# A hybrid delta-rule and attention layer: Q/K norm and turn written later, squares moved to GpSimd, clearing products, two loads reordered

## Chip, cores and metric

One core of a Trainium2 chip runs the whole layer. The metric is the device time of one execution in microseconds (us), the median over several runs; the 128-partition engines are TensorE (PE; its weight loads are PEld), VectorE (DVE), ScalarE (ACT), GpSimd (POOL) and SyncE (SP), which issues most of the DMAs.

## What is computed

The input x is 2048 tokens of 1024 float32 values. It is normalised and multiplied by one wide matrix; the columns feed a gated delta rule (four heads of 128) and a dilated attention (eight heads of 64, three dilations); both are gated, concatenated, multiplied by an output matrix and added to x. Cut to the parts that the change touches:

```python
def rms_norm(x, w):
    xf = x.astype(jnp.float32)
    return xf * lax.rsqrt(jnp.mean(xf * xf, axis=-1, keepdims=True) + EPS) * w.astype(jnp.float32)

def dilated_attention_branch(qkv, gate, q_norm_w, k_norm_w, rel_bias):
    q, k, v = jnp.split(qkv, 3, axis=-1)
    q = rms_norm(split_heads(q, ATT_HEADS), q_norm_w) * (ATT_HEAD_DIM ** -0.5)
    k = rms_norm(split_heads(k, ATT_HEADS), k_norm_w)
    ...
    return o * jax.nn.silu(gate.astype(jnp.float32))

def hybrid_layer(x, norm_w, w_in, ...):
    h = rms_norm(x, norm_w).astype(x.dtype)
    proj = h @ w_in
    ...
    return x + mixed @ w_out
```

## The kernel before

**Products in three parts.** Every projection is done as three products of split operands: a rounded high part (`xh`, `wh`) and the rest (`xl`, `wl`). ACT makes the high parts, DVE the rests by a subtraction of two tiles in SBUF.

**The opening (lines 218 to 342).** The first column block is multiplied as the data come in, in eight rounds, one for each 128 rows of x (`kt`). In a round ACT makes `xh` and one or two `wh` and squares the x tile (`x_square`, lines 256 to 264); DVE makes `xl` (`x_low`), one or two `wl` (`z_low`) and adds the square to the running sum `acc` (`x_add`); PE does twelve products into four banks of PSUM (`pz`); SP issues the next loads. `x_square` is used for all four blocks of 512 tokens (`tb`); in the opening it works on block 0. POOL does one small power at line 226 and is then free until the sums of squares are raised to -1/2 (`x_norm`, line 291). Everything from line 218 to line 379 is pinned: each engine gets its instructions in the order in which they are written.

**The middle (lines 380 to 778)** is not pinned. A planner puts the instructions of the projections, the triangular inverses and the delta rule in order by their priorities (`PATT0`, `PGATE` and the like) and by its own account of times; each engine's order is fixed when the program is built.

**The Q, K and V projection (`proj_fill`, lines 881 to 955)** is a generator that writes one product per call, 2304 in all, counted by `n`. Two token tiles share one bank of the ring `pj`, which has two (`PJB`), so a bank takes 48 products, and the product 48 after its end is the first to need the same bank again. For Q and K, three things follow the last product of a bank: `post_sums` at once (ACT squares, DVE sums, and POOL adds and raises `ss` to -1/2), `post_norm` 24 products later (DVE reads the bank, multiplies by `ss` and so frees it), and `post_turn` another 18 later (PE turns four 128x128 tiles into the single bank `pm`, ACT scales them, two DMAs of the ACT queue write them out). This part is pinned too. Its first 960 products are taken before the attention starts and are planned in among the delta rule; the others are written between the pieces of the attention, nine, nine and eight per step (`step`, lines 1275 to 1287). A step also writes DVE's work on scores, copies and weights; POOL's queue holds the reordering of keys and queries (`keys`, `queries`) and the blending of the three patterns (`blend`), in the order written.

**The output projection (`out_fill`, lines 1354 to 1442)** is the generator for steps 48 to 97. Its jobs are numbered; `load` (line 1370) issues a job's load ahead, and for attention parts only once `ready` has the quarter that it needs, which line 1266 adds at a step and a place in it. `res_load` at lines 1427 to 1429 brings back, for the last five token tiles, the sums that were stored earlier. All of these are issues on SP's queue, which waits in order.

The line of a product or of an ACT instruction in a pinned part is 99 in the profile, that of the helper which writes them; such rows are told apart by their tiles.

Of the kernel before, what the change touches and what calls it, by code (L numbers as in the profile page):

```python
# [16 lines left out]
P = 128  # L17
# [67 lines left out]
def hybrid(tc, xT, x, norm_w, w_in, conv_w, a_log, dt_bias, dn_norm_w, q_norm_w, k_norm_w,  # L85
# [135 lines left out]
    adma = nc.scalar.dma_start  # L221
    adma(nw, norm_w)
    nc.vector.memset(one, 1.0)
    warm = sp0.tile([P, 4], F32, name="warm")
    nc.scalar.activation(warm, mhalf[:, :4], AF.Silu)
    nc.gpsimd.tensor_tensor(warm, phalf, mhalf[:, :4], op=ALU.pow)
# [29 lines left out]
    def x_square(n):  # L256
        tb, kt = divmod(n, KT)
        if kt == 0:
            acc[tb] = sp0.tile([P, 512], F32, name="acc", bufs=2)
            nc.scalar.activation(acc[tb], xraw[n], AF.Square)  # L260
        else:
            sq = sp0.tile([P, 512], F32, name="sq", bufs=2)
            nc.scalar.activation(sq, xraw[n], AF.Square)
            acc[tb, kt] = sq

    def x_low(n):
        tb, kt = divmod(n, KT)
# [76 lines left out]
    n = KT  # L344
# [536 lines left out]
    def proj_fill():  # L881

        raws = w_load(0)
        cur = w_split(raws[0]) + w_split(raws[1])
        posts = []
        n = 0
        for s_ in range(12):
            hf, i = divmod(s_, 6)
            g2, w = SETS[i]
            nxt = []  # L890
            for o8 in range(8):
                tt = hf * 8 + o8
                if o8 % 2 == 0:
                    ps = psA.tile([P, 512], F32, name="pj", bufs=PJB)

                nx = s_ * 8 + o8 - 44
                if nx in (0, 4):
                    alloc_x(2 + nx // 4, xp0)
                if nx == -4:
                    for k in range(3):  # L900
                        x_load(k)
                if nx == -1:
                    x_load(3)
                    x_load(4)

                if s_ < 11:
                    if o8 == 1:
                        raws = w_load((i + 1) % 6)
                    if o8 == 5:
                        nxt = w_split(raws[0])  # L910
                else:
                    if o8 == 1:
                        rs = [w_out_load(k) for k in range(2)]
                    if o8 == 4:
                        wo_tiles(0)
                    if o8 >= 4:
                        wo_split(o8 - 4, rs[o8 - 4])
                        if o8 < 6:
                            rs.append(w_out_load(o8 - 2))
                tb, o = divmod(tt, 4)  # L920
                c0 = tt % 2 * 256
                for kt in range(KT):
                    if 0 <= nx < 8 and kt % 4 == 0:
                        k = 2 * nx + kt // 4
                        x_split(k)
                        if k < 11:
                            x_load(k + 5)
                    for x_, w_ in ((xh, 0), (xh, 1), (xl, 0)):
                        while posts and posts[0][0] <= n:
                            posts.pop(0)[1]()  # L930
                        if s_ < 11 and o8 == 7 and kt == 2 and w_ == 0 and x_ is xh:
                            nxt += w_split(raws[1])
                        m = nc.tensor.matmul(ps[:, c0:c0 + 256], x_[tb][:, kt, o * P:(o + 1) * P],
                                             cur[kt][w_][:, cur[kt][2], :256], start=kt == 0 and x_ is xh and w_ == 0,
                                             stop=kt == KT - 1 and x_ is xl)
                        if n == HOLD * 192:
                            tc.add_manual_dep(m.ins, mark["pe"].ins.name, NOSYNC, reason="behind the delta rule")
                        n += 1
                        yield
                if tt % 2:  # L940
                    t0 = tt - 1
                    if w == 2:
                        post_v(g2, t0, ps)
                    else:
                        ss = post_sums(t0, ps)

                        def norm(ps=ps, ss=ss, w=w, g2=g2, t0=t0):
                            qn = post_norm(ps, ss)
                            posts.append((n + 18, lambda: post_turn(w, g2, t0, qn)))
                            posts.sort(key=lambda a: a[0])  # L950
                        posts.append((n + 24, norm))
                        posts.sort(key=lambda a: a[0])
            cur = nxt
        while posts:
            posts.pop(0)[1]()
# [278 lines left out]
    def at_step(t, where, f, *args):  # L1234
        todo.setdefault((t, where), []).append((f, args))
# [3 lines left out]
    for i, g in enumerate(G):  # L1239
        b = 12 * i  # L1240
        if i:
            at_step(b - 4, 1, g["load"])
        at_step(b - (2 if i else 3), 1, g["queries"], 0)
        for k in range(1, 6):
            at_step(b + 2 * k - 3, 0, g["queries"], k)
        at_step(b, 0, g["keys"], 1)
        at_step(b + 4, 0, g["keys"], 2)
        for j, t, where in (((0, -1, 0), (2, 1, 0), (4, 3, 0), (5, 4, 0), (6, 6, 0), (7, 7, 2), (8, 8, 0), (10, 10, 0))
                            if i < 4 else
                            ((0, 0, 0), (2, 1, 2), (4, 3, 2), (5, 4, 0), (6, 6, 0), (7, 7, 2), (8, 8, 0), (9, 9, 2),  # L1250
                             (10, 10, 0), (11, 11, 2))):
            at_step(b + t, where, g["vload"], j)
        at_step(b + 12, 1, g["sums"])
        at_step(b + 12, 2, g["sums_out"])
        if i < 7:
            at_step(b + 13, 2, g["sums_back"], 0, dma)
            at_step(b + 14, 0, g["sums_back"], 1, dma)
            at_step(b + 15, 1, g["weigh"])
            at_step(b + 15, 2, g["weigh2"])
            at_step(b + 16, 0, g["factors"])  # L1260
            for qd in range(4):
                d = i < 6
                at_step(b + 16 + qd + d, 0 if d else 2, g["blend_load"], qd)
                at_step(b + 17 + qd + d, 0 if d else 1, g["blend"], qd, nc.gpsimd)
                at_step(b + 19 + qd + d, 0 if d else 1, g["mixed"], qd)
                at_step(b + 20 + qd + 2 * d, 0, ready.add, (i // 4, i % 4, qd))
        else:
            at_step(b + 13, 0, g["sums_back"], 0, dma)
            at_step(b + 13, 1, g["sums_back"], 1, dma)
# [84 lines left out]
    def out_fill():  # L1354
# [48 lines left out]
        for i, (tt, kind, n, mm, buf) in enumerate(jobs):  # L1403
            if mm is None:
                continue
            nth += 1
            first, last = mm
            todo_ = []
            while i + 1 + len(todo_) < len(jobs):
                todo_.append(i + 1 + len(todo_))  # L1410
                if jobs[todo_[-1]][3]:
                    break
            if first:
                res = RES[tt] if kind == "att" else res_load(tt, x)
                po = [None, None]
            m = 0
            for b in range(2):
                if first:
                    po[b] = psX.tile([P, 512], F32, name="po", bufs=3)
                for _ in products(po[b], ops, b, first, last):  # L1420
                    m += 1
                    if nth < 2 and m in (8, 16):
                        k = 2 * nth + m // 8 - 1
                        wo_split(4 + k, RAW[k])
                    if m >= 3 * n and m % 3 == 0 and todo_:
                        nxt = split(todo_.pop(0))
                    if nth in range(18, 23) and m == 3 * n + 8:
                        k = nth - 18
                        RES[Q2[k]] = res_load(Q2[k], acc_d, K0[:, k * D:(k + 1) * D] if k < 2 else None)
                    if m >= 4:  # L1430
                        load(i + 3 if nth < 24 else i + 5)
                    if m == 3 * n + 4 and store:
                        dma(*store)
                        store = None
                    yield
                if last:
                    cs_ = slice(b * 512, (b + 1) * 512)
                    nc.vector.tensor_tensor(res[:, cs_], po[b], res[:, cs_], op=ALU.add)
            assert not todo_
            ops = nxt  # L1440
            if last and not (kind == "att" and n == 3):
                store = ((out if kind == "att" else acc_d)[tt * P:(tt + 1) * P, :], res)
# [77 lines left out]
```

## Time and profile before

| what | value |
|---|---|
| median of 3 runs | 1446.1 us (1442.88 to 1447.8) |
| the profiled execution, own time | 1442.2 us |
| its span, first to last instruction | 1440.4 us |
| busy: PE / DVE / ACT / POOL | 1374.0 / 897.2 / 680.1 / 427.2 us |
| mean granted clock of TensorE | 0.987 of full speed |
| chain that ended last, by engine | PE 61%, DVE 15%, DMA 11%, ACT 5%, issue 4%, POOL 2% |

The profiled execution lies 3.9 us under the median of the runs, so sums are made against its 1442.2 us and then carried to the median. In rows of the timeline the first number is the start and the second the duration, both in us; x4 is a count of merged instructions, and a bracket holds the idle time of the engine before the row and what ended it.

### The profile page before, as it was taken

What the parts mean: (1) busy time and instruction counts of PE and PEld (TensorE: products, weight loads), DVE (VectorE), ACT (ScalarE), POOL (GpSimd) and SP (SyncE); (2) the same over time, 40 slices, a digit from 0 to 9 for tenths busy, and PEclk for the clock granted to TensorE, in tenths of its full rate; (3) what the DMA queues carried; (4) which work ended last, traced back from release to release, by engine and by line L of the source; (5) the groups of instructions that cost most, each with busy time, mean ns of one, the idle gap of its engine ahead of it and who ended that gap; (6) DMA issues with size and microseconds to landing.
All of it is one profiled execution on the core that took longest, in us unless ns stands there. A gap on an engine that the chain in (4) does not pass through costs nothing.

```text
span 1440.4 us, 28745 instructions
## 1 busy us (share of the span) xinstructions
PE 1374.0 (95%) x10234; PEld 1223.6 (85%) x10234; DVE 897.2 (62%) x2786; ACT 680.1 (47%) x1937; POOL 427.2 (30%) x499
## 2 busy tenths in 40 slices
PE   7999999999998998999999899999998999999988
PEld 7998777777877887999999889999887778888877
DVE  6526678799894365777777554544354645466455
ACT  7634436642221333444444476665555545555520
POOL 0000000000002112442432523657466274655500
PEclk9999999999999999999999999999998999999999
DMA  7653445773557556566554554464448574755764
GB/s 218 165 117 70 99 102 133 156 132 55 116 88 193 147 83 171 133 166 168 133 143 76 124 127 116 100 174 119 112 118 246 146 247 134 216 154 171 200 175 150
DMA packets 301154, 205.00 MB, mean 142 GB/s; under 512 B 149283, under 2 KB 271027, under 8 KB 300500
## 3 DMA queue, kind: packets, MB, share of 16 engines
q1 hardware_dynamic: 233924, 171.70, 48.6%
q10 hardware_dynamic: 67088, 31.47, 7.9%
q8 instruction: 81, 1.33, 0.4%
q14 instruction: 61, 0.50, 0.1%
HBM read 142.61 MB, written 60.50 MB: 141 GB/s over the span
## 4 chain that ended last, share of the span: by engine, by line
PE 61%; DVE 15%; DMA 11%; ACT 5%; issue 4%; POOL 2%; SPq 1%; ACTq 0%; DVEq 0%; POOLq 0%
PE pj L99 13%; PE po L99 8%; PE pz L99 5%; PE sc L99 5%; PE pj L206 4%; PE pj L207 4%; PE pj L208 4%; PE pv L99 3%; PE pt L99 3%; DVE cy L473 3%; DVE inv L540 2%; DMA kT<-cv 2%; PE C L714 2%; PE SU L720 2%; ACT pr L99 2%
## 5 line engine op out<-in xcount | busy, mean ns | idle before, releaser
L99 ACT ACTIVATE pr<-pr,ml 128x192 f32<-128x192 f32 (+2 forms) x384 | 156.8, 410 | 161.6 <-DVE ml L99 161.6
L99 PE MATMUL pj<-wh,xh 128*128 128x256 f32 (+1 forms) x776 | 227.7, 293 | 0.0
L99 PE MATMUL pj<-wl,xh 128*128 128x256 f32 (+1 forms) x776 | 227.6, 293 | 0.0
L99 PE MATMUL pj<-wh,xl 128*128 128x256 f32 (+1 forms) x776 | 225.8, 291 | 0.0
L208 PE MATMUL pj<-xh,wl 128*128 128x512 f32 x512 | 203.9, 398 | 3.6 <-DVE wl L192 3.6
L206 PE MATMUL pj<-xh,wh 128*128 128x512 f32 x512 | 203.9, 398 | 1.3 <-ACT cy L475 1.2
L207 PE MATMUL pj<-xl,wh 128*128 128x512 f32 x512 | 203.2, 397 | 0.0
L99 PEld LDWEIGHTS pj<-wl,xh 128*128 128x128 f32 x776 | 148.3, 191 | 0.6 <-issue 0.4
L99 PEld LDWEIGHTS pj<-wh,xl 128*128 128x128 f32 x776 | 148.3, 191 | 0.0
L99 PEld LDWEIGHTS pj<-wh,xh 128*128 128x128 f32 x776 | 148.1, 191 | 0.2
L99 DVE CUSTOM_DVE_ANT_0 pr<-sc,bias 128x192 f32<-128x192 f32 (+2 forms) x384 | 100.1, 307 | 71.0 <-PE sc L99 70.2
L208 PEld LDWEIGHTS pj<-xh,wl 128*128 128x128 f32 x512 | 96.6, 189 | 27.3 <-DVE wl L192 5.3
L206 PEld LDWEIGHTS pj<-xh,wh 128*128 128x128 f32 x512 | 96.8, 189 | 24.4 <-ACT cy L475 1.6
L473 DVE SCALAR_TENSOR_TENSOR cy<-cu,cw,cy 128x512 f32<-128x512 f32 x144 | 107.9, 752 | 15.2 <-ACT cy L471 13.6
L207 PEld LDWEIGHTS pj<-xl,wh 128*128 128x128 f32 x512 | 96.6, 189 | 21.9
L99 POOL COPY qz<-q 64x512 f32<-64x512 f32 x96 | 92.5, 964 | 57.7 <-PE sc L99 54.7
L657 POOL MEMSET at__4520<- 64x256 f32 x1 | 0.3, 304 | 354.5 <-PE pj L207 354.5
L99 DVE COPY pT<-pt 64x128 f32<-64x128 f32 (+2 forms) x220 | 69.3, 323 | 56.4 <-PE pt L99 53.1
L99 PE MATMUL po<-xh,mhh 128*128 128x512 f32 x212 | 88.8, 419 | 3.9 <-ACT mhh L99 3.9
L99 PE MATMUL pv<-pT,V 128*64 128x128 f32 (+1 forms) x1328 | 79.1, 269 | 9.8 <-DVE pT L99 4.7
L99 PE MATMUL po<-xl,mhh 128*128 128x512 f32 x212 | 88.1, 415 | 0.0
L99 PE MATMUL po<-xh,mhl 128*128 128x512 f32 x212 | 87.7, 414 | 0.3 <-DVE mhl L99 0.3
(360 smaller groups left out, 3151.8 us busy)
## 6 DMA issues: line engine op xcount, KB each, us to landing
wraw<-in_w_in SPq DMA_DIRECT2D x44, 512.0 KB, 6.9
cv<-cy ACTq DMA_DIRECT2D x48, 256.0 KB, 2.7
Fb<-F SPq DMA_DIRECT2D x64, 192.0 KB, 5.7
xr<-in_xT SPq DMA_DIRECT2D x32, 256.0 KB, 4.5
kT<-cv SPq DMA_DIRECT2D x32, 256.0 KB, 3.3
qk<-qs ACTq DMA_DIRECT2D x64, 128.0 KB, 3.3
res<-in_x SPq DMA_DIRECT2D x13, 512.0 KB, 5.2
V<-v_d SPq DMA_DIRECT2D x20, 256.0 KB, 6.2
```

The lines of the kernel that those rows point to most:

```text
L99: i = f(*args, **kw)
L206: nc.tensor.matmul(ps, wh[:, k, c * P:(c + 1) * P], xh[tb][:, kt, :], start=kt == 0, stop=False)
L207: nc.tensor.matmul(ps, wh[:, k, c * P:(c + 1) * P], xl[tb][:, kt, :], start=False, stop=False)
L208: nc.tensor.matmul(ps, wl[:, k, c * P:(c + 1) * P], xh[tb][:, kt, :], start=False, stop=kt == KT - 1)
L473: nc.vector.scalar_tensor_tensor(y, u[:, i:i + 512], cw[:, ct, i:i + 1], y, op0=ALU.mult, op1=ALU.add)
L540: nc.vector.tensor_tensor(pr_[:, :i, :i], Tt[:, :i, :i], L[:, None, :i, i].to_broadcast([P, i, i]), op=ALU.mult)
L657: nc.gpsimd.memset(at_[:CH, :, :CH], 0.0)
L714: nc.tensor.matmul(pc[:, s_], g["WQ"][:, u, s_], S0[:, s_], start=True, stop=True)
L720: nc.tensor.matmul(su[:, s_], g["Ks"][:, u, s_], VN, start=True, stop=True)
```

## The change

Five edits. (1) DVE clears 128 columns of `rstd_b`, and 14 products of these zeros by themselves go into a bank of PSUM at the start, into no result. (2) `x_square` runs on POOL for block 0, eight squares in all, and on ACT for the others as before. (3) In `proj_fill` the norm is written 30 products after the bank's end, where it was 24, and the turn 24 after the norm, where it was 18. (4) For the last head pair but one (`i == 6`) `ready` is added at the end of the step before, three products earlier. (5) The fifth of the reloads of stored sums is written at the 24th job of the output projection (`nth` 23), where it was at the one before.

```diff
     nc.vector.memset(one, 1.0)
+    nc.vector.memset(rstd_b[:, :P], 0.0)
+    pm = psA.tile([P, 512], F32, name="pm", bufs=1)
+    for _ in range(14):
+        nc.tensor.matmul(pm[:, :P], rstd_b[:, :P], rstd_b[:, :P], start=True, stop=True)
...
         if kt == 0:
-            acc[tb] = sp0.tile([P, 512], F32, name="acc", bufs=2)
-            nc.scalar.activation(acc[tb], xraw[n], AF.Square)
+            acc[tb] = sq = sp0.tile([P, 512], F32, name="acc", bufs=2)
         else:
-            sq = sp0.tile([P, 512], F32, name="sq", bufs=2)
+            acc[tb, kt] = sq = sp0.tile([P, 512], F32, name="sq", bufs=2)
+        if tb == 0:
+            nc.gpsimd.tensor_tensor(sq, xraw[n], xraw[n], op=ALU.mult)
+        else:
             nc.scalar.activation(sq, xraw[n], AF.Square)
-            acc[tb, kt] = sq
...
-                            posts.append((n + 18, lambda: post_turn(w, g2, t0, qn)))
+                            posts.append((n + 24, lambda: post_turn(w, g2, t0, qn)))
                             posts.sort(key=lambda a: a[0])
-                        posts.append((n + 24, norm))
+                        posts.append((n + 30, norm))
...
-                at_step(b + 20 + qd + 2 * d, 0, ready.add, (i // 4, i % 4, qd))
+                at_step(b + 20 + qd + 2 * d - (i == 6), 0 if i < 6 else 2, ready.add, (i // 4, i % 4, qd))
...
-                    if nth in range(18, 23) and m == 3 * n + 8:
-                        k = nth - 18
+                    if nth in (18, 19, 20, 21, 23) and m == 3 * n + 8:
+                        k = min(nth - 18, 4)
```

## Rows read from the trace of the kernel before

**Rows 1.** Busy by stretch: length, PE, PEld, DVE, ACT, POOL (counts), clock, DMA share, GB/s
```profile
12.25:22.57 10.32, 9.40 (x66) 8.27 (x65) 9.32 (x19) 8.59 (x19) 0.00 (x0) 1.00 0.86 270
22.57:108.50 85.93, 85.92 (x719) 85.83 (x720) 39.52 (x78) 44.69 (x84) 5.17 (x4) 1.00 0.61 147
```

**Rows 2.** Timeline of the opening: ACT, two products of PE, the last round.
```profile
6.04 0.72 ACT L99 ACTIVATE xh<-xr,nw 128x512 fp32r<-128x512 f32 x1 [1.26 <-DMA xr<-in_xT]
...
8.64 0.42 PE L99 MATMUL pz<-wh,xh 128*128 128x260 f32 x1
...
12.91 0.28 PE L99 MATMUL pz<-wh,xl 128*128 128x260 f32 x1
...
21.78 0.74 DVE L99 SCALAR_TENSOR_TENSOR xl<-xr,nw,xh 128x512 fp32r<-128x512 f32 x1
...
22.57 0.39 PE L99 MATMUL pz<-wh,xl 128*128 128x260 f32 x1 [0.27 <-DVE xl L99]
```

**Rows 3.** Groups by shape, 6.8 to 22.6 us, DVE and ACT: busy us, mean ns.
```profile
L99 DVE SCALAR_TENSOR_TENSOR xl<-xr,nw,xh 128x512 fp32r<-128x512 f32 x8 | 6.0, 747 | 1.6 <-ACT xh L99 1.6
L99 DVE TENSOR_TENSOR acc<-acc,sq 128x512 f32<-128x512 f32 x7 | 4.8, 689 | 1.0 <-ACT sq L99 1.0
L99 DVE TENSOR_TENSOR wl<-wraw,wh 128x260 fp32r<-128x260 f32 x11 | 4.3, 424 | 1.5 <-ACT wh L99 1.5
...
L99 ACT ACTIVATE sq<-xr 128x512 f32<-128x512 f32 x7 | 4.3, 615 | 0.0
```

**Rows 4.** Groups by shape, whole span, POOL with two tiles read.
```profile
L99 POOL TENSOR_TENSOR gt<-gt,Fb 128x256 f32<-128x256 f32 x28 | 20.6, 734 | 2.2
...
L99 POOL TENSOR_TENSOR ss<-ss,e 128x8 f32<-128x8 f32 x32 | 7.7, 240 | 197.3 <-DVE ss L99 173.1 <-DVE ml L99 23.9
```

**Rows 5.** Groups by shape, 400 to 811 us, DVE: the split of a weight tile.
```profile
L99 DVE TENSOR_TENSOR wl<-wraw,wh 128x1024 fp32r<-128x1024 f32 x12 | 14.6, 1217 | 1.0 <-ACT wh L99 1.0
```

**Rows 6.** Timeline at 990 us: that split on DVE, and POOL beside it.
```profile
990.85 1.81 DVE L99 TENSOR_TENSOR wl<-wraw,wh 128x1024 fp32r<-128x1024 f32 x1 [1.78 <-ACT wh L99]
...
990.72 0.86 POOL L99 TENSOR_TENSOR Fb<-Fb,op 128x256 f32<-128x256 f32 x1
991.65 1.59 POOL L99 TENSOR_TENSOR Fb<-Fb 128x256 f32<-128x256 f32 x1
```

**Rows 7.** Waits from 811 to 1105 us, PE and DVE: total us, times, longest.
```profile
PE pm L99 <- DVE t L99: 10.2, 6, 2.9
PE pv L99 <- DVE pT L99: 3.7, 2, 3.0
...
DVE t L99 <- POOL ss L99: 9.3, 5, 4.0
```

**Rows 8.** Timeline of two of the six turns that wait: PE, and DVE's norm.
```profile
856.20 0.66 PE L99 MATMUL pm<-cs,t 128*128 128x128 f32 x4 [1.92 <-DVE t L99]
857.38 1.53 PE L99 MATMUL pv<-pT,V 128*64 128x128 f32 x24
...
1015.31 0.69 DVE L99 TENSOR_TENSOR t<-pj,ss 128x512 f32<-128x512 f32 x1 [4.01 <-POOL ss L99]
...
1016.06 1.12 PE L99 MATMUL pm<-cs,t 128*128 128x128 f32 x4 [2.92 <-DVE t L99]
1017.83 1.80 PE L99 MATMUL sc<-C,qz 128*128 128x64 f32 x8
```

**Rows 9.** Busy by stretch, columns as in rows 1, after the longest of these waits.
```profile
1015.90:1022.70 6.80, 6.64 (x35) 6.42 (x37) 2.12 (x12) 2.60 (x10) 2.37 (x5) 0.50 0.95 187
```

**Rows 10.** Timeline near the end: SP's queue and PE.
```profile
1381.06 0.48 SPq L99 DMA_DIRECT2D res<-acc_d  x1
1381.58 0.96 SPq L99 DMA_DIRECT2D mt<-mx_d  x2
...
1386.18 0.50 PE L99 MATMUL po<-xh,mhh 128*128 128x512 f32 x1 [3.18 <-ACT mhh L99]
```

**Rows 11.** Timeline of PE in the delta rule: a wait for a load.
```profile
545.47 1.09 PE L675 MATMUL A<-cs,vT 128*128 128x128 f32 x4 [6.74 <-DMA vT<-cv]
```

## The prediction

> **What bounds the kernel.** I read the page first: PE is busy for 1374.0 of 1440.4 us, so the end moves only with time in which PE stands, waits or runs at half its clock. Then the busy times by stretch, to find where that is. From 22.57 to 108.5 us PE has no gap (85.92 of 85.93 us, 719 products, so 0.12 us each) [rows 1]: what shifts the start of that stretch shifts everything behind it. Before it stands the opening, which ends when the last `xl` is made (21.78 + 0.74 = 22.52 us) and PE starts the last round at 22.57 [rows 2]. There DVE is the busiest but for PE itself, which takes in its time only what the others hand it: 9.32 of 10.32 us [rows 1]. The waits of 811 to 1105 us come next: PE stood 10.2 us, in six waits, before turns, for DVE's norm, and DVE stood 9.3 us before norms for POOL's `ss` [rows 7]. Last the timeline near the end, where PE stands 3.18 us for a split of a late `mt` [rows 10].
>
> The sum is made against the profiled execution's 1442.2 us; the median of the runs is 3.9 us above it, 1446.1, and what the edits are worth is carried to that. About 0.3% (4.3 us) is what a measurement of this kernel can tell from no change.
>
> **Clearing products.** A product of 260 columns lasts 0.42 us early in the opening and 0.28 us later [rows 2]; the 14 products are to have PE at its later pace when the first data come. Their cost: four turns of the same 128 columns took 0.66 us at the later pace [rows 8], so 14 take between 14 x 0.66 / 4 = 2.3 and twice that, 4.6 us; they start as soon as DVE has cleared the columns, and the first real product needs the `xh` that begins at 6.04 [rows 2], which leaves 1.4 us for that clearing at the worst. The loads hide them; without that cover they would cost up to 4.6. Their gain: in the last round PE waits for DVE, not for itself [rows 2], so I take 0.
>
> **First squares on POOL.** ACT loses eight squares of 0.615 us [rows 3], POOL gets them. If nothing else happened, the last `xh` would come two squares earlier (the one ahead of it and what had piled up), and the opening would end some 1.3 us sooner. But DVE's three instructions of the opening each read two tiles in SBUF, and so does POOL's square. The trace shows what such a pair does [rows 6]: a weight split that lasts 1.22 us in the mean where POOL works little [rows 5] lasts 1.81 beside POOL, ending only after POOL's first instruction (991.58) has ended; and POOL's next one, 0.73 alone [rows 4], takes 1.59 and ends 0.6 us after DVE's. Both engines' work went one after the other: of DVE's 1.22 us, POOL's 2.52 us (990.72 to 993.24) less 0.86 and 0.73, that is 0.93, could not be shared, or 76%.
> Price of a square: no row has POOL multiply 512 columns. Upper end, two of 256: 1.47. Lower end, from 0.20 for the smallest instruction of its kind (240 ns in the mean of 32, some stretched) and 0.73 for 256, in proportion: 0.20 + 2 x 0.54 = 1.28 [rows 4]. I take 1.38, the middle, as both ends come from the same kind; eight are 11.0 us. DVE's share up to the last `xl`: 6.0 + 4.1 (six of the seven sums) + 4.3 = 14.4 us [rows 3], of which 76% to all excludes POOL: 10.9 to 14.4. Laid end to end from the first x tile (6.04), the last `xl` ends between 6.04 + 21.9 = 27.9 and 6.04 + 25.4 = 31.4, where it ended at 22.52: 5.4 to 8.9 us later. POOL also runs while DVE has nothing to do yet, at the start of the opening, where the first square lies. I take +6, near the lower end, which the row itself gives.
> [...]
>
> **Norm and turn later.** 32 norms and 32 turns move, each turn with its four PE transposes, one ACT scaling and two DMAs of the ACT queue. The first reader of what those DMAs write is a load after 576 products, and the last turn that it needs now comes at product 384 + 54 = 438, so no load waits for it. The norm moves 6 products, the turn 12. But the bank that the norm frees is needed by the product 48 behind its end, and the turn stood at 42: when DVE or POOL is late, PE now stops at 48 in place of 42. So a wait shrinks by six products (0.7 us) and by whatever attention lies between them, not by twelve.
> The longest: PE stopped at 1013.14, the norm ended at 1016.00 [rows 8]. Six products and the piece of scores (1.80 at half clock, about 1.0 at full) bring PE to 1014.9; 1.1 us stay, 1.8 are gained. The first: stopped at 854.28; six products and the 1.53 us of values bring it to 856.5, after the norm: 1.92 gained [rows 8]. The other four hold 10.2 - 2.9 - 1.9 = 5.4 us; 0.7 each is 2.8. In sum 6.5. What is late next is DVE: PE also waits for its copies of weights (3.7 us) [rows 7], and POOL, for which the norm waited 4.01 us, is as busy as before. I take half, 3.3.
> After the longest wait PE ran 6.80 us at a clock of 0.50, that is at 1.2 GHz [rows 9], and it had stood 2.92 us before it fell. If only 1.1 us of that wait stay I take the stretch as gone: 3.4 us back. Together -6.6; ends: -10 (all 6.5 and the clock), 0 (the wait reappears at the bank, the clock falls all the same and DVE is held up as long).
> DVE's order gains too: while the norm waits for POOL, copies queued behind it wait; six products later some of these are ahead of it. I put nothing on it.
>
> **Reordered last loads.** SP issues the reload of a stored sum (512 KB) just before the `mt` that PE then lacks [rows 10]. Moved behind, it gives the `mt` its 0.48 us of the queue, and the transfer no longer shares the DMA engines with it. I take 1.2 us in all; ends: 0.5 (the queue alone) and 3.2 (the whole wait). The reload is used at the last job, with a job of 18 products between, so it is not missed. `ready` three products earlier puts an `mt` ahead of a load of `V` on SP's queue, where it waits for its store to land; `V` is used two steps later. I put 0 on that.
>
> **Sum.** +6.0 - 6.6 - 1.2 = -1.8: 1442.2 becomes 1440.4, and 1446.1 becomes 1444.3. That is within what can be told apart.
>
> **Rivals.**
> *The squares fit.* POOL's square reads one tile twice and the DVE instructions are short; were they not shut out by each other, the opening ends 1.3 us sooner: -1.3 - 6.6 - 1.2 = -9.1, 1437.0. For it speaks that DVE stands in the opening at times (1.6 + 1.0 + 1.5 us [rows 3]); against it stands the split beside POOL [rows 6]. Chance 0.24.
> *The wait moves to the bank.* PE stops at product 48 as long as it did at 42, but for the six products between; the clock still falls. Then the norms give 6 x 0.7 = 4.2, of which half as above, and no more: +6.0 - 2.1 - 1.2 = +2.7, 1448.8. It decides at every old wait of over 0.7 us, unless attention lies between the two places. Chance 0.10.
> *The planner lays the middle anew.* Of the 32 norms and turns the first 16 are planned in among the delta rule, between 505 and 811 us. PE has one long wait there, 6.74 us for a load of `vT` [rows 11]. One more such wait, with a stretch of half clock behind it (3.4, [rows 9]), costs 10.1: -1.8 + 10.1 = +8.3, 1454.4, slower. It decides if a load is put behind a waiting one on SP's queue by more than PE has products in hand. Chance 0.10; nothing in the edits touches a load there.
>
> **Numbers.** My forecast has 0.56: of it 0.34 lie within 0.3%, 0.12 below (norms at their upper end) and 0.10 above (the lock at its upper end). Faster: 0.24 + 0.12 = 0.36. Same: 0.34 + 0.10 = 0.44. Slower: 0.10 + 0.10 = 0.20. The range takes the squares' rival (1437.0) in and the planner's out, and above it reaches the lock's 8.9 with the norms at half of what I took: +8.9 - 3.3 - 1.2 = +4.4, 1450.5. The forecast's own range is 1441 to 1450.5, its lower end with the norms' 10 us.
>
> **What would show it.** Right: squares of about 1.4 us on POOL, `xl`, `wl` and sums of the opening stretched, PE's first stretch without a gap beginning near 28.5 us, not 22.6; PE's waits at turns gone, one or two at the first product of a bank, no half clock near 1016; the wait near 1386 shorter by 1.2 us. Wrong: an opening that ends before 22 us, or DVE's instructions there at their old durations.

## Result and profile after

The changed kernel takes 1433.98 us in the median (1433.75 to 1434.53), the kernel before beside it 1444.78: a ratio of 0.9928, 95% interval 0.9903 to 0.9954, or 10.8 us less where 1.8 were forecast. The time lies under the forecast's range. The profiled executions show only 7.7 us of it (1442.2 and 1434.53): that of before lies 2.6 us under its median, that of the changed kernel 0.6 over.

The page of the changed kernel, its head:

```profile
span 1432.6 us, 28797 instructions
...
PE 1376.4 (96%) x10262; PEld 1224.8 (85%) x10262; DVE 905.4 (63%) x2787; ACT 677.1 (47%) x1929; POOL 438.4 (31%) x507
```

**The opening got longer, by less than forecast.** Busy times by stretch (PE, PEld, DVE, ACT, POOL, clock, DMA share, GB/s), to be read against [rows 1]:

```profile
12.25:22.57 10.32, 6.41 (x40) 5.18 (x41) 10.32 (x15) 4.35 (x9) 4.47 (x4) 1.00 0.76 230
22.57:26.20 3.63, 2.96 (x24) 2.64 (x23) 3.63 (x7) 3.50 (x9) 1.16 (x1) 1.00 0.40 98
26.20:112.13 85.93, 85.93 (x720) 85.84 (x720) 39.51 (x78) 42.26 (x79) 5.17 (x4) 1.00 0.60 148
```

DVE is now busy for the whole 10.32 us with 15 instructions where it had done 19, and PE did 40 products in place of 66. PE's stretch without a gap begins at 26.20 instead of 22.57, and is as dense as before. The timeline of the opening shows why:

```profile
1.13 5.70 PE L99 MATMUL pm<-rstd_b 128*128 128x128 f32 x28 [1.13 <-DVE rstd_b L99]
6.58 0.37 PE L99 MATMUL pz<-wh,xh 128*128 128x260 f32 x1
...
5.71 1.04 POOL L99 TENSOR_TENSOR acc<-xr 128x512 f32<-128x512 f32 x1 [1.94 <-DMA xr<-in_xT]
8.23 1.04 POOL L99 TENSOR_TENSOR sq<-xr 128x512 f32<-128x512 f32 x1 [1.48 <-DMA xr<-in_xT]
10.01 1.45 POOL L99 TENSOR_TENSOR sq<-xr 128x512 f32<-128x512 f32 x1 [0.74 <-DMA xr<-in_xT]
...
20.45 1.16 POOL L99 TENSOR_TENSOR sq<-xr 128x512 f32<-128x512 f32 x1 [1.63 <-DVE acc L99]
22.84 1.16 POOL L99 TENSOR_TENSOR sq<-xr 128x512 f32<-128x512 f32 x1 [1.23 <-DVE acc L99]
...
17.50 1.60 DVE L99 TENSOR_TENSOR wl<-wraw,wh 128x260 fp32r<-128x260 f32 x2
...
20.29 0.42 DVE L99 TENSOR_TENSOR wl<-wraw,wh 128x260 fp32r<-128x260 f32 x1
20.63 1.52 DVE L99 SCALAR_TENSOR_TENSOR xl<-xr,nw,xh 128x512 fp32r<-128x512 f32 x1
...
25.41 0.74 DVE L99 SCALAR_TENSOR_TENSOR xl<-xr,nw,xh 128x512 fp32r<-128x512 f32 x1
```

The `xl` at 20.63 has POOL's square beside it, which ends at 21.61; it takes 1.52 us, where the last one, with nothing beside it, takes 0.74. It ends 0.54 us after the square, so 0.54 / 0.74 = 73% of it did not run beside the square. POOL in turn waits 1.63 us in a round for DVE to free one of the two tiles of squares: the two engines pass the turn to and fro. All eight squares (the first one makes `acc`) end before the last `xl` begins. The groups by shape from 6.8 to 26.2 us, beside [rows 3]:

```profile
L99 POOL TENSOR_TENSOR sq<-xr 128x512 f32<-128x512 f32 x7 | 8.3, 1183 | 9.0 <-DVE acc L99 6.7 <-DMA xr<-in_xT 2.2
L99 DVE TENSOR_TENSOR wl<-wraw,wh 128x260 fp32r<-128x260 f32 x11 | 7.6, 722 | 1.0 <-ACT wh L99 1.0
L99 DVE SCALAR_TENSOR_TENSOR xl<-xr,nw,xh 128x512 fp32r<-128x512 f32 x8 | 7.6, 944 | 1.0 <-ACT xh L99 1.0
```

**The waits at turns are gone, and two smaller ones stand at the bank.** Waits from 811 to 1105 us (total us, times, longest), beside [rows 7]:

```profile
PE pv L99 <- DVE pT L99: 5.1, 2, 4.5
PE pj L99 <- DVE t L99: 2.3, 1, 2.3
...
PE pj L99 <- DVE ml L99: 1.3, 1, 1.3
...
DVE t L99 <- POOL ss L99: 6.5, 2, 4.2
```

The row of six waits for `pm`, 10.2 us, has no successor; 2.3 + 1.3 = 3.6 us stand at the first product of a bank (products 1968 and 1296, both multiples of 48). The larger of the two in the timeline, and the stretch behind it:

```profile
1013.57 0.20 POOL L99 TENSOR_TENSOR ss<-ss,e 128x8 f32<-128x8 f32 x1
1013.86 1.65 POOL L99 TENSOR_TENSOR ss<-ss,mhalf 128x8 f32<-128x8 f32 x1
...
1015.54 0.69 DVE L99 TENSOR_TENSOR t<-pj,ss 128x512 f32<-128x512 f32 x1 [4.16 <-POOL ss L99]
...
1016.28 0.56 PE L99 MATMUL pj<-wh,xh 128*128 128x256 f32 x1 [2.30 <-DVE t L99]
...
1016.28:1023.00 6.72, 6.72 (x50) 6.32 (x51) 1.78 (x11) 3.71 (x13) 5.41 (x6) 0.75 0.91 198
```

POOL's power ends, DVE's norm runs, the bank is free, PE goes on: the same chain as at the old longest wait [rows 8]. The mean granted clock is 0.75 over the 6.72 us behind it (3.4 us of them at 0.50, that is 1.2 GHz, the others at full clock), where it was 0.50 over 6.80 [rows 9].

**At the end** the two loads of `mt` now stand ahead of the reload on SP's queue, and the wait for the split is 1.9 us in place of the 3.18 of [rows 10]:

```profile
1374.30 0.97 SPq L99 DMA_DIRECT2D mt<-mx_d  x2
1375.31 0.48 SPq L99 DMA_DIRECT2D res<-acc_d  x1
1376.81 0.51 ACT L99 CAST mhh<-mt 128x384 fp32r<-128x384 f32 x1 [5.47 <-DMA mt<-mx_d]
...
PE po L99 <- ACT mhh L99: 1.9, 1, 1.9
```

### The profile page after: what moved, and what is told of

It reads as the page before. It is cut to its first block, busy times and chain, and to the rows that moved or that the text cites. A ratio compares the mean times of both kernels' runs of the same rounds, so it can differ in the third digit from the quotient of the medians.

```text
span 1432.6 us, 28797 instructions
## 1 busy us (share of the span) xinstructions
PE 1376.4 (96%) x10262; PEld 1224.8 (85%) x10262; DVE 905.4 (63%) x2787; ACT 677.1 (47%) x1929; POOL 438.4 (31%) x507
## 4 chain that ended last, share of the span: by engine, by line
PE 66%; DVE 14%; DMA 9%; ACT 4%; issue 4%; SPq 1%; POOL 1%; ACTq 0%; DVEq 0%; POOLq 0%
PE pj L99 15%; PE po L99 9%; PE sc L99 6%; PE pz L99 5%; PE pv L99 4%; PE pj L206 4%; PE pj L207 4%; PE pj L208 4%; PE pt L99 4%; DVE cy L478 3%; DVE inv L545 2%; DMA kT<-cv 2%; PE C L719 2%; PE SU L725 2%; DVE inv L547 2%
## 5 line engine op out<-in xcount | busy, mean ns | idle before, releaser
L99 POOL TENSOR_TENSOR Fb<-Fb,op 128x256 f32<-128x256 f32 x84 | 70.6, 854 | 60.8 <-DMA Fb<-F 59.7
```

The costliest lines, as they stand in the source:

```text
L99: i = f(*args, **kw)
```

## The experiments

All runs by stretch, from one profile each, in us. Opening: the end of the last `xl`. Middle: from there to product 960 of the Q, K and V projection (counted from 0), where the delta rule ends. Attention: from there to the first product of the output projection proper. Rest: to the end of the span. The last column is for how much of the attention the clock was granted at 0.50 (half clock, 1.2 GHz); half of that is taken as time lost, an estimate: products of the projection begin every 0.21 us there and every 0.12 at full clock.

| kernel | opening | middle | attention | rest | at half clock |
|---|---|---|---|---|---|
| before | 22.5 | 776.7 | 307.3 | 333.9 | 12.2 |
| g1, before again | 23.6 | 776.9 | 307.0 | 335.6 | 10.2 |
| g2, quarter alone | 23.0 | 778.0 | 307.4 | 336.4 | 12.2 |
| g3, reload alone | 22.8 | 775.6 | 305.6 | 330.9 | 10.2 |
| e4, both load edits | 22.7 | 774.7 | 306.3 | 332.8 | 10.2 |
| e2, opening's edits | 26.0 | 779.9 | 301.9 | 334.3 | 3.4 |
| e3, norms and turns | 23.1 | 772.6 | 294.1 | 334.9 | 0 |
| f1, those of the attention | 22.8 | 777.1 | 296.3 | 333.6 | 5.3 |
| f2, turns alone | 23.2 | 777.8 | 295.3 | 335.0 | 3.4 |
| f4, norms, turns, loads | 22.8 | 773.6 | 299.9 | 330.9 | 13.7 |
| e1, after, squares on ACT | 23.7 | 776.2 | 295.9 | 330.3 | 3.4 |
| h2, the same again | 22.1 | 774.6 | 296.0 | 335.0 | 3.4 |
| f3, after, POOL writes only | 21.7 | 773.6 | 297.7 | 333.9 | 10.2 |
| h3, last squares later | 22.0 | 775.7 | 296.8 | 329.3 | 6.8 |
| g4, sums without POOL | 23.3 | 779.6 | 309.9 | 340.1 | 22.8 |
| after | 26.1 | 775.6 | 298.6 | 332.2 | 6.8 |
| h1, after again | 26.1 | 774.5 | 295.4 | 333.5 | 3.4 |

### Each part by itself

**e1**, the changed kernel with block 0's squares back on ACT:

```diff
-        if tb == 0:
-            nc.gpsimd.tensor_tensor(sq, xraw[n], xraw[n], op=ALU.mult)
-        else:
-            nc.scalar.activation(sq, xraw[n], AF.Square)
+        nc.scalar.activation(sq, xraw[n], AF.Square)
```

> The changed kernel with the eight squares back on ScalarE, all else as changed. Theory A (the squares on GpSimd cost the opening 3.6 us, since GpSimd and VectorE shut each other out, and PE starts its unbroken stretch that much later): the last xl ends near 22.5 us in place of 26.15, every later landmark comes 3.6 us earlier, the whole is 1429 to 1431 us. Rival B (the opening's delay is made up behind it, so the squares cost nothing in the end): 1433 to 1435 us.

1427.95 us, ratio 0.9891 (0.9873 to 0.9910), the opening at 23.7. That is under theory A's range; carried by its ratio to the 1444.78 of the first result it is 1429.0, A's lower end. B falls.

**e2**, the kernel before with the clearing products and the squares on POOL (edits 1 and 2 of the diff).

> The kernel before with the clearing products and the squares on GpSimd alone. Theory A: 3 to 4 us slower than the kernel before, near 1448 us, with the unbroken stretch of PE beginning near 26.2 us. Rival B: no slower than 1445 us. Clearing products: PE at 0.12 us a product from its first real product on, without a gain in the end.

1445.33 us, ratio 1.0019 (1.0003 to 1.0035); the opening ends at 26.0. By its ratio it is 2.7 us slower (0.4 to 5.1), which lies between A and B. The six waits at turns are all there:

```profile
PE pm L99 <- DVE t L99: 8.8, 6, 2.9
```

So the opening's edits lose, and do it without touching the turns.

**e3**, the kernel before with edit 3 alone.

> The kernel before with the later norm and turn alone. Theory A: the waits before turns are gone, 811 to 1105 us gets some 8 to 9 us shorter, the whole is 1434 to 1437 us; the longest wait stands at the first product of a bank near 1012 us. Rival C (the middle, planned anew, gives most of the gain): 505 to 811 us is over 3 us shorter and the attention gains under 6. Rival D (my forecast, waits reappear behind DVE): 1438 to 1441 us.

1431.36 us, ratio 0.9913 (0.9894 to 0.9932): 12.6 us of before's 1442.99. Carried to 1444.78 it is 1432.2, a little under A's range. D, the forecast, falls. So does C: its middle is 4.1 us shorter, but the attention 13.2. PE's waits in the attention are, at the bank, those of the changed kernel:

```profile
PE pv L99 <- DVE pT L99: 3.8, 2, 3.2
PE pj L99 <- DVE t L99: 2.2, 1, 2.2
PE sc L99 <- DVE ml L99: 2.1, 2, 1.1
PE pj L99 <- DVE ml L99: 1.3, 1, 1.3
```

PE's wait for copies of weights (`pT`), which was to be late next, is 3.8 us where it was 3.7 [rows 7]; in the changed kernel's own profile it is 5.1.

**e4**, the kernel before with edits 4 and 5.

> The kernel before with the two reordered loads alone. Theory A: PE's wait of 3.2 us for the split of the late mt falls to 1.9, the whole is 1.0 to 1.5 us shorter, 1443.5 us. Rival E (the earlier ready also shortens 1105 to 1365 us, where the changed kernel is 2.2 us shorter): 1441 to 1442 us.

1439.48 us, ratio 0.9979 (0.9963 to 0.9995), 3.0 us (0.7 to 5.3). PE's wait for the split is 1.3 us, under A's 1.9. The three parts alone come to 2.7 - 12.6 - 3.0 = -12.9 us; together they gave -10.8, which their intervals allow.

### Where the norms' gain comes from

**f1**, late norms and turns only for the part between the pieces of the attention:

```diff
-                            posts.append((n + 18, lambda: post_turn(w, g2, t0, qn)))
+                            posts.append((n + (24 if n > 960 else 18), lambda: post_turn(w, g2, t0, qn)))
...
-                        posts.append((n + 24, norm))
+                        posts.append((n + (30 if n > 930 else 24), norm))
```

> The kernel before with norm at 30 and turn at 24 behind it only for the banks that end at product 960 or later, that is those written between the pieces of the attention; the earlier ones, which the planner lays in among the delta rule, stay at 24 and 18. The run with all norms later gained 11.6 us, of which its profile shows 3.6 at the end of the delta rule. Theory A, the gain is the six waits of the attention (10.2 us, of which 3.5 come back at the bank) and the half clock behind them: product 960 within 1 us of before, 8 to 10 us gained by the last product of the projection, ratio 0.992 to 0.995. Rival, the gain is that the planner lays the middle anew, and the attention only moves with it: ratio 0.997 or above.

1432.9 us, ratio 0.9932 (0.9908 to 0.9955). The attention is shorter by 11.0 us, the middle is as before (777.1). So the attention's part carries the gain; what the planned half adds (0.9913 with it) is within the intervals.

**f2**, the norm left at 24, the turn 30 behind it:

```diff
-                            posts.append((n + 18, lambda: post_turn(w, g2, t0, qn)))
+                            posts.append((n + 30, lambda: post_turn(w, g2, t0, qn)))
```

> The kernel before with the norm where it was, 24 products behind the bank, and the turn 30 behind the norm, at product 54 as in the change. Theory A1, what counts is that PE comes to the turn later: the waits for DVE's norm before turns go, the bank is freed as early as before, the waits at the first product of a bank (1.3 and 2.2 us with the norm at 30) are no longer than those; ratio as with both later, 0.990 to 0.993. Rival A2, what counts is DVE's order, copies of weights no longer queued behind a norm that waits for POOL: then leaving the norm at 24 gives at most half, ratio 0.995 or above, and DVE waits for POOL's ss some 9 us again, where it was 6.4 with the norm at 30.

1432.58 us, ratio 0.9923 (0.9900 to 0.9947), not told apart from e3: the norm's own move gained nothing that can be measured. Its waits in the attention:

```profile
PE pv L99 <- DVE pT L99: 4.0, 2, 3.3
PE pj L99 <- DVE t L99: 2.9, 2, 2.0
...
DVE t L99 <- POOL ss L99: 9.1, 2, 5.3
```

DVE stands 9.1 us for POOL, as in the kernel before, and the gain is there all the same: what counts is that PE comes to the turn later, not that DVE's order is better. A2 falls. PE's waits at the bank are 2.9 us with the norm at 24 and 3.5 with it at 30.

**g4**, the kernel before, where the sums of squares don't go through POOL:

```diff
-        nc.gpsimd.tensor_tensor(ss.rearrange(...), ..., op=ALU.add)
-        nc.gpsimd.tensor_tensor(ss, ss, mhalf, op=ALU.pow)
+        nc.vector.tensor_scalar(ss, ss, 1e-3, 0.125, op0=ALU.mult, op1=ALU.add)
```

> The kernel before, norms and turns where they were, but the sums of squares of Q and K go from DVE to DVE by one small scaling, and POOL's addition and power are left out (so Q and K are not normalised by the right factor). Theory, the waits at turns come from POOL's queue, in which the power stands behind blending and copies: without it DVE's 9.3 us of waiting and most of PE's 10.2 us at turns go although nothing is written later, product 960 to the first product of the output projection is shorter by 7 to 10 us, ratio 0.991 to 0.994. Rival, DVE's own order makes the norm late: PE's waits at turns stay at 7 us or more, ratio 0.997 or above.

1450.2 us, ratio 1.0042 (1.0010 to 1.0073), which neither theory had. Waits in the attention:

```profile
PE pv L99 <- ACT pT L99: 4.2, 1, 4.2
PE pv L99 <- DVE pT L99: 4.0, 3, 3.0
PE pm L99 <- DVE t L99: 3.5, 3, 2.1
```

DVE's row of waits for POOL is gone and the waits at turns fell from 10.2 to 3.5 us, so POOL's queue did make those norms late. But a wait of 4.2 us that before does not have stands at 947 us (ACT's queue held behind its DMA issues), and 22.8 us of the attention run at half clock in place of 12.2: the stretch is 2.6 us longer, not 7 to 10 shorter, and the middle, which the planner lays anew, is 2.9 longer. Taking POOL out is no substitute for writing the turn later. Why ACT's queue stood there was not followed further.

### What POOL's squares collide with

**f3**, the changed kernel with a write of a constant in place of each square:

```diff
-            nc.gpsimd.tensor_tensor(sq, xraw[n], xraw[n], op=ALU.mult)
+            nc.gpsimd.memset(sq, 1.0)
```

> The changed kernel with the eight squares of block 0 on POOL replaced by eight writes of a constant into the same tiles (the sums of squares of block 0 are left out; DVE's sums still wait for them). Theory of the lock, POOL's reads of SBUF shut DVE's two-input instructions out: without them the splits of 260 columns go back from 1.59 to 0.42 us or 0.77 beside other work, and the last xl ends at 23 to 24 us, as with the squares on ACT (23.7), not at 26.1. Rival, DVE waits because POOL's result comes late or because POOL writes: the splits stay stretched or DVE waits for POOL, and the last xl ends near 26.

1428.84 us in one run; this kernel leaves out the sums of squares of block 0. (The 1.59 us expected for a split are two splits in one row; one took 0.72 in the mean.) Groups by shape, 6.8 to 22.6 us, and two rows of the timeline:

```profile
L99 DVE SCALAR_TENSOR_TENSOR xl<-xr,nw,xh 128x512 fp32r<-128x512 f32 x8 | 6.0, 750 | 1.4 <-ACT xh L99 1.4
L99 DVE TENSOR_TENSOR acc<-acc,sq 128x512 f32<-128x512 f32 x7 | 4.8, 688 | 0.0
L99 DVE TENSOR_TENSOR wl<-wraw,wh 128x260 fp32r<-128x260 f32 x11 | 4.3, 426 | 1.9 <-ACT wh L99 1.9
L99 POOL MEMSET sq<- 128x512 f32 x5 | 2.6, 526 | 10.5 <-DVE acc L99 10.5
...
16.17 0.53 POOL L99 MEMSET sq<- 128x512 f32 x1 [1.42 <-DVE acc L99]
...
16.36 0.75 DVE L99 SCALAR_TENSOR_TENSOR xl<-xr,nw,xh 128x512 fp32r<-128x512 f32 x1
```

DVE's means are those of [rows 3] to within 3 ns (426 against 424), though POOL writes the same tiles and still waits for DVE; the `xl` at 16.36 has a write beside it to 16.70 and keeps its 0.75 us. So it is not POOL's writing that stretches DVE's instructions. What is left is the reading; that POOL also multiplies in a square was not tried apart from it. The opening ends at 21.7, before all those with squares on ACT in the loop (22.1 to 23.7).

### The loads

**g1**, the kernel before unchanged.

> The kernel before once more, unchanged, for a second profile of the same order of instructions. The profiles so far differ at product 960, the end of the delta rule, by up to 6 us either way (opening taken off: 1.0 us less to 4.1 less, and 2.3 more). If that comes from the order that the planner lays, this profile agrees with the first within 0.5 us there. If it comes from the execution, it differs by 1 us or more, and those differences are no effect of any edit.

1445.13 us in one run. The middle took 776.9 us against 776.7, the attention 307.0 against 307.3; in between the two profiles were apart by up to 1.7 us, the opening by 1.1 and the rest by 1.7. Two more kernels have two profiles each, and these lie further apart: the changed kernel and h1 by 3.2 us in the attention, e1 and h2 by 4.7 in the rest. A difference of this size in one stretch of one profile shows no effect.

**g2** and **g3** split the load edits; g2 has only the line of `ready`, g3 only those of `nth`.

> The kernel before with only the last quarter of head pair 6 added three products earlier. The prediction gave it 0. If it is worth nothing, the stretch from product 500 of the output projection to product 560 is as long as before (23.5 us) and PE still waits some 3 us for the split of the late load; if it carries part of the 3.0 us of both load edits, that stretch is shorter by 1 us or more.

> The kernel before with only the fifth reload of a stored sum written one job later. The prediction gave it 1.2 us (0.5 for the queue alone, 3.2 for the whole wait): the stretch from product 500 of the output projection to product 560 is 22.3 us where before has 23.5, and PE's wait for the split of the late load is 1.9 to 2.0 us, not 3.2. Rival, the wait is set by the transfer of the stored part itself: unchanged at some 3 us.

g2 took 1446.59 us and g3 1436.75, one run each. PE's waits of the end, first of g2:

```profile
PE po L99 <- ACT mhh L99: 3.3, 1, 3.3
```

and of g3:

```profile
PE po L99 <- ACT mhh L99: 1.2, 1, 1.2
PE po L99 <- DVE mhl L99: 0.3, 1, 0.3
```

With the quarter alone products 500 to 560 of the output projection took 23.5 us (before 23.4), with the reload alone 20.9. The reload carries the gain, 2.5 us in this pair of profiles. Over all profiles it is less: PE's wait for `mhh` is 3.2 to 4.2 us in the seven that have the reload early (g4 apart) and 1.2 to 2.2 in the nine that have it late, and the sixty products take 23.6 and 21.9 us in the mean, 1.7 less.

### Is there a better version, and what do the squares cost at the end?

**f4**, the kernel before with edits 3 to 5: no clearing, squares on ACT.

> The kernel before with norms and turns later and the last loads reordered, without the clearing products and with the squares on ACT. If the edits add up, norms 12.6 and loads 3.0 as each had alone: ratio 0.989, 1427.5 us where before has 1443. If the clearing products gained something in the run that had them with the squares on ACT (0.9891), this one is slower than that one by it, 0.990 or above.

1429.08 us, ratio 0.9909 (0.9882 to 0.9937). The expectation took 0.990 or above as a sign that the clearing products gain, and the ratio lies there; but its interval overlaps with that of e1, and the opening, where the gain would have to be, ends at 23.7 and 22.1 us with them (e1 and h2) and at 22.5 to 23.6 without. So no gain is shown.

**h1**, **h2** and **h3** ran in one set of rounds: the changed kernel, the same with e1's edit, and f4 with the last three squares behind the opening's loop:

```diff
-        x_square(kt)
-        x_add(kt)
+        if kt < 5:
+            x_square(kt)
+            x_add(kt)
...
-        x_in(kt + XRB)
+        if kt < 5:
+            x_in(kt + XRB)
...
+    for kt in range(5, KT):
+        x_square(kt)
+        x_add(kt)
+        x_in(kt + XRB)
```

> The changed kernel once more, on the same chip and in the same rounds as the two after it, so that what squares on POOL cost is read from one comparison. Expected as first measured: ratio 0.991 to 0.995, and its profile again with the last xl near 26.1 us.

> The changed kernel with the squares of block 0 on ACT, as before the change. If the 2.5 to 3.6 us by which the last xl comes earlier reach the end, this median is 2 to 5 us under that of the changed kernel in the same rounds. Rival, the opening is paid back later, at the 6.8 us waits of the middle: within 1 us of it.

> Norms and turns later and the last loads reordered, no clearing products, squares of block 0 on ACT, the last three of them (with their sums on DVE and the loads that reuse their x tiles) written behind the opening's loop. If ACT's squares delay the last xh and DVE's sums the last xl, the last xl ends near 21.7 us, as where no square was made on ACT, 0.8 to 1.4 us earlier than with all squares in the loop (22.5 to 23.7), and PE stays unbroken behind it: the median is at or up to 2 us below that of the run with all squares on ACT. Rival, the data arrive no sooner, and the loads written later hold the next block up: the last xl at 22.5 or later, or PE waits before 110 us; equal or slower.

1430.93 (ratio 0.9928, 0.9908 to 0.9948), 1429.41 (0.9913, 0.9889 to 0.9937) and 1429.23 us (0.9914, 0.9894 to 0.9935). Last `xl` of the opening in h1, then in h2:

```profile
25.35 0.74 DVE L99 SCALAR_TENSOR_TENSOR xl<-xr,nw,xh 128x512 fp32r<-128x512 f32 x1
```

```profile
21.40 0.74 DVE L99 SCALAR_TENSOR_TENSOR xl<-xr,nw,xh 128x512 fp32r<-128x512 f32 x1
```

The opening ends 25.35 + 0.74 = 26.09 in the one and 22.14 in the other, 3.95 us apart, but the medians differ by 1.5 us only, under the 2 to 5 expected, and e1 had 3.7 less by ratio (0.0037 of 1443 = 5.3, on another chip). The six runs of h1 and the six of h2 overlap, and their difference alone is not clear of noise; in e2 the squares and the clearing products together cost 0.4 to 5.1 us. So the squares cost up to some 5 us at the end, and how much is open. h3 ends its opening at 22.0, h2 at 22.1, and two profiles of one kernel lie 1.6 apart there (e1 and h2): neither the expected gain nor the rival's late end is seen, and the medians are 0.2 us apart. e1, f4, h2 and h3 all have medians under that of the changed kernel, by 1.5 and 1.7 us where they ran beside it; none is shown to be faster than it.

## Why the prediction was wrong

With profiles of one kernel up to 5 us apart in a stretch, the terms are best read from means over the table. The opening: 26.1 with squares on POOL (three profiles), 22.9 with all of them on ACT in the loop (eleven, g4 apart), +3.1. The middle: 774.5 with the norms late there (eight), 777.0 without (seven, f2 and g4 apart), -2.4. The attention: 296.7 with norms and turns late (nine), 305.9 without (six, g4 apart), -9.2. The rest: 332.1 with the reload later (nine), 334.8 without (seven, g4 apart), -2.7. So +6.0 became +3.1, -6.6 became -9.2 with -2.4 in the middle beside it, and -1.2 became -2.7. The sum is -11.2, and -10.8 was measured. The same means say what the shorter stretches are made of. PE's waits in the attention come to 18.5 us without the later turns and to 11.6 with them, -6.9; in the rest they are 1.7 us less, in the middle the same (21.6 and 21.5). The time at half clock, halved, is 1.9 us less in the attention, 1.6 in the middle and 1.3 in the rest. So about 4.8 us of the gain are clock by this estimate, where the forecast had 3.4, and all of those behind the longest wait.

**Clearing products: right.** They took 5.70 us, more than the upper end of 4.6 (each of the 14 stands as two in the trace, x28), but began at 1.13, and the first real product started at 6.58 (6.82 before); the last round waited for DVE as before, and no gain is seen.

**Squares on POOL, "I take +6, near the lower end": the term was mis-sized, +3.1 to +3.6.** The mechanism was right: DVE's opening instructions stretched, PE's unbroken stretch late, and the share of an `xl` that could not be shared 73% where the weight split gave 76% [rows 6]. Wrong was the price of a square. All eight lie ahead of the last `xl`, as laid out, but two take 1.04 us, one 1.45 and five 1.16, not 1.38: 9.3 in place of 11.0. With that the lower sum becomes 6.04 + 9.3 + 10.9 = 26.2, where 26.15 was measured. The other 0.6 us are the step from the lower end, 5.4, to 6. That the sum then fits so closely is in part luck: POOL also waits up to 1.63 us between two squares, which is no term of it. By the Trainium skill ("SBUF — State Buffer", section "Who interferes with whom") a GpSimd instruction that only writes does not contend with a VectorE instruction that reads two tiles in SBUF; f3 agrees (426 ns beside 424).

**Norm and turn later, "I take half, 3.3": the step that failed most.** The waits in full came near what was worked out: 6.5 us were to go, and 10.2 - 3.6 = 6.6 went. Place by place that is in part luck: at the longest wait 1.1 us were to stay and 2.3 did, at the first nothing stays, as said, and the other four gave 4.1 where 2.8 were expected. The term failed because these 6.5 were halved: DVE or POOL would be late next. They were not, but for one place (a wait of 0.49 us at 867.43 became one of 1.31 at the bank, where DVE's norm stands behind a split): PE's wait for copies is 4.0 us in the mean of the six profiles without the later turns and 4.2 in that of the nine with them, and f2 shows that DVE may stand as long for POOL as before while PE's waits shrink. Of the attention's 9.2 us, 1.9 are the clock (half clock 9.7 us in the mean of those six, 5.9 in the mean of the nine, half of the difference), where I took 3.4, and 6.9 are the waits, where I took 3.3. That the middle would move by -2.4 was no term at all. f1 against e3 leaves open whether it is one, but the traces show one place: a wait of 1.0 to 2.0 us near 750 us (the delta rule's `C` for DVE's `o`) stands in all seven profiles with the early norms there, with 3.4 or 6.8 us at half clock behind it in four, and in none of the eight with the late ones. In g1 and in the changed kernel, 735 to 765 us:

```profile
PE C L714 <- DVE o L732: 1.5, 1, 1.5
```

```profile
PE A L699 <- ACT tmp L690: 0.8, 1, 0.8
```

**Last loads, -1.2: right in kind and a little small.** In the changed kernel the wait fell by 1.3 us; alone the reload gave 2.5. Over all profiles the rest is 2.7 us shorter, of which 1.7 are the wait, inside the ends of 0.5 and 3.2, and 1.3 the clock, by the estimate above. In the one profile of g2 `ready` shows no gain, as said.

**The rivals.** *The squares fit* forecast a time near the result (1437.0) for a reason that is false: the squares don't fit. That it came nearer than the forecast is luck. *The wait moves to the bank* has its mechanism, at 869.93 and 1016.28 us, but for 3.6 us, not the whole. *The planner lays the middle anew* did not come: the wait for `vT` is 6.64 us in the changed kernel, where it was 6.74, and PE's waits of the middle together are as long as before in the mean.

## What to carry to other kernels

Where an engine only collects a result that another one makes, write the collecting as late as the next user of its space allows, and price the gain by the full shrinkage of each wait, until a trace shows what would be late next; halving for caution cost more here than any other step, 3.3 to 3.6 us. Before moving work to GpSimd ask what VectorE reads from SBUF at that moment: beside subtractions of two tiles most squares on GpSimd took 1.16 us each, most of it in VectorE's way, where ACT made it in 0.62 beside VectorE. When edits gain and lose at once, run each alone: of five here one gave most, one a little, one lost, and two did nothing that can be measured.

## What the runs showed beside that

The same wait at the bank, 2.0 to 2.3 us long, was followed by no stretch at half clock in e1, e3, f1, h1 and h3, by 3.4 us of it in the changed kernel, f2, f3 and h2, and by 6.8 us in f4. e1 and h2 are one kernel, and so are the changed kernel and h1; in each pair one profile has that stretch and the other has not, with waits of 2.22 and 2.22, 2.30 and 2.22 us. So the edits do not decide it, and clock time lost behind a single wait is a chance, not a fixed price. Between the profiles of late-norm kernels the half clock of the attention ranges from 0 to 13.7 us, up to 6.8 us in time. Seven of the eight squares of 512 columns on POOL cost 2.0 to 2.3 ns per column, where the products of two 256-column tiles of [rows 4] cost 2.9: the nearest row was not a good price.
